# Quarter-array recurrence, u parts made two steps ahead, and other counts around the gate stage in a hybrid encoder kernel

## The chip, the cores and the metric

The kernel runs on one core of one Trainium2 chip. The metric is the time of one execution on the device, in microseconds. The parts of the core are called as in the profile: PE (TensorE, matrix products), PEld (its weight loads), DVE (VectorE), ACT (ScalarE), POOL (GpSimd), SP (SyncE, which here only issues transfers).

## The reference

The reference is two residual layers over 512 tokens of width 1024, with a final norm. Each layer has a mixer and a feed-forward part. What the change touches is in the two feed-forward parts and in the second layer's mixer.

The feed-forward part picks, per token and head, 16 of 16384 single-neuron experts, and adds them:

```python
top_s, pos = lax.top_k(cand.astype(jnp.float32), PEER_TOPK)
idx = jnp.take_along_axis(cand_idx, pos, axis=-1)
gate = jax.nn.softmax(top_s, axis=-1)
...
act = jax.nn.gelu(jnp.einsum('thkd,td->thk', u, xb), approximate=False)
out = jnp.einsum('thk,thkd->td', gb * act, ve)
```

Half of the second mixer is a recurrence per head (8 heads of 64), with a 64 x 64 state:

```python
def step(state, inp):
    r_t, w_t, k_t, v_t, kk_t, a_t = inp
    sa = jnp.einsum('bhvk,bhk->bhv', state, kk_t)
    state = (state * w_t[:, :, None, :] - sa[..., None] * (kk_t * a_t)[:, :, None, :]
             + v_t[..., None] * k_t[:, :, None, :])
    y = jnp.einsum('bhvk,bhk->bhv', state, r_t)
    return state, y
```

## The kernel before

The program is even mixer, feed-forward (`peer`, layer 0), odd mixer, `peer` (layer 1). Each engine carries out its instructions in the order of the program; what stands first and waits holds up all behind it on that engine.

**The feed-forward part** computes for 384 of the 512 tokens all 16384 experts densely, in 128 tiles of 128 experts: a "u tile" (`u_mm`, L1379) is 24 products of 128x128 by 128x384, three per slice of the contraction. The weights `ur` and the tokens are split into a high part and a low part (`uh`, L1369, made on ACT by L151; `ul`, L1376, on DVE), and `mm3` (L179) runs high by high (L182), high by token-low (L183) and low by token-high (L184). The result goes through a gelu on ACT into `act` tiles that stay, or into `acts` tiles (two buffers) that go out to memory (`ad`, the spill). The first `NB_ACT` = 15 tiles stay, the next `NB_SPILL` = 38 are spilled; the others come later. The 128 tokens that are left get their expert rows by indirect transfers (`g_fetch`, `g_work`).

While the u tiles run, DVE finds the best 16 (`level2`) and builds for the dense tokens the gates: per block of 16 tokens one-hot arrays `ohC`, `ohA`, and two `ohB` (L1606, four operations of 128x2048), which PE multiplies (`flush`, L1589, `gps`); ACT copies the result, and it is written to memory (`gd`). `background` (L1615) yields the cost of each piece, and a loop (L1633) puts in a `u_step` for every `G_STEP` = 4.2 of cost: it makes the low part of tile j + 1, loads the high part of tile j + 2, and multiplies tile j. When the gates are done (or up to `NB_LAST` tiles ahead of the end), the remaining tiles follow until 53 - 2, then the v stage opens and the last two run. This stretch is called the gate stage here, and the passage from the last gates to the first v product the handover.

**The v stage** (L1645 on) goes over the 128 tiles with 18 products each (`v_mm`, L1701, outputs `o`), weights split into `vh` and `vl`, and activations times gates (`Hf`, then `Hh` and `Hl`). The gates of 8 tiles are read back in one transfer `gt` (1536 KB). In the first 38 steps the spilled activations are read back (`a_load`), in the next 75 each step also makes one more u tile, and the last steps are v products alone. `units` (L1822) spreads the row work over these steps.

**The recurrence** (`odd_mixer`, L1106 to L1275) works on 8 chunks of 64 tokens. Two heads lie on the 128 partitions. Each operand is expanded to a block-diagonal 128x128 matrix with zeros beside the two heads' blocks (`expand`, L719, mostly on POOL), and `mm4` (L1114) runs four full 128x128 products for the four pairs of heads. `prep(c)` (L1118) makes for one chunk the inverse of a triangular matrix from blocks of 16 (`Xc`, `XTc`) by two levels, and the products that don't need the state; `step(c)` (L1187) runs the chain through the state: `psT` to `t1`, `psU` to `u`, `psS` to the new state, and `psY` to the output. `prep(c + 1)` and a group norm of chunks before are woven into the steps (L1259 on).

Of the kernel before, what the change touches and what calls it, by code (L numbers as in the profile page):

```python
# [25 lines left out]
P = 128  # L26
# [67 lines left out]
for _nm, _c in (("blk64", 128), ("mB", 128), ("mK", 256), ("lv16", 128), ("lv32", 128), ("hm", 2), ("rows", 4)):  # L94
    OC[_nm] = (_n, _c)
    _n += _c
# [3 lines left out]
def odd_const_array():  # L100
    c = np.zeros((P, NOC), np.float32)
    i = np.arange(P)
    r, q = i[:, None], i[None, :]
    same = r // 64 == q // 64
    rr, qq = r % 64, q % 64

    def put(nm, a):
        o, n = OC[nm]
        c[:, o:o + n] = a

    put("blk64", same / 64.0)
    put("mB", np.where(q < 64, 1.0 * (rr < qq), -1.0 * (rr <= qq)))
    put("mK", np.concatenate([same & (rr < qq), same & (rr <= qq)], 1))
    put("lv16", same & (rr // 32 == qq // 32) & (rr % 32 < 16) & (qq % 32 >= 16))
    put("lv32", same & (rr < 32) & (qq >= 32))
    put("hm", np.stack([i < 64, i >= 64], 1))
# [550 lines left out]
def odd_mixer(k):  # L667
# [8 lines left out]
    with ExitStack() as st:  # L676
# [40 lines left out]
        hm = o_("hm")  # L717

        def expand(e, dst, src):  # L719

            if e is nc.scalar:
                for h in range(2):
                    k.act(dst[:, :, 64 * h:64 * h + 64], src, AF.Copy, scale=hm[:, h:h + 1])
                return
            e.tensor_tensor(dst.rearrange("p a (h t) -> p a h t", h=2), src[:, :, None, :].to_broadcast([P, 4, 2, 64]),
                            hm[:, None, :, None].to_broadcast([P, 4, 2, 64]), op=ALU.mult)

        def gram(c, pb):
            tt = slice(64 * c, 64 * c + 64)
            b0 = pb.tile([P, 4, P], F32, name="b0", tag="b0", bufs=2)  # L730
            expand(nc.gpsimd, b0, be[:, :, tt])

            def rest():
                ps = bank4()
                for p in range(4):
                    mm(ps[:, p, :], b0[:, p, :], AR[:, p, :, tt], start=True, stop=True, skip_group_check=True)
# [10 lines left out]
        with ExitStack() as s1:  # L747
# [136 lines left out]
            with ExitStack() as s2:  # L884
# [40 lines left out]
                def grams(n):  # L925
                    if n >= 4:
                        gq.pop(0)()
                    if 2 <= n < 10:
                        gq.append(gram(n - 2, p3))
# [28 lines left out]
        def bc4(a):  # L958
            return a[:, None, :].to_broadcast([P, 4, P])

# [143 lines left out]
        for i in range(3):  # L1104
            ws.fetch(i)
        rs = ExitStack()  # L1106
        pw = rs.enter_context(sb("odw", 2))
        S, C = {}, {}
        Y = AR[:, :, 1]

        def t4(nm, n=1, bufs=2):
            return pw.tile([P, 4, n * P], F32, name=nm, bufs=bufs)

        def mm4(ps, l, r, start, stop):  # L1114
            for p in range(4):
                mm(ps[:, p, :], l[:, p, :], r[:, p, :], start=start and p == 0, stop=stop, skip_group_check=True)  # L1116

        def prep(c):  # L1118
            tt = slice(64 * c, 64 * c + 64)
            K0, B0 = t4("k0"), t4("b0")  # L1120
            AR0 = t4("ar", 2)
            X, XT = t4("x"), t4("xt")
            N1, N2 = t4("n1"), t4("n2", bufs=1)
            NB2 = t4("nb2")

            def level(dst, nm):
                for h in range(2):
                    f = slice(64 * h, 64 * h + 64)
                    (nc.vector if h and not c else nc.gpsimd).tensor_tensor(dst[:, :, f].rearrange("p a (b i) -> p a b i", b=4),
                                            Na[:, :, :, 4 * c:4 * c + 4].rearrange("p i b a -> p a b i"),  # L1130
                                            o_(nm)[:, None, f].rearrange("p a (b i) -> p a b i", b=4)
                                            .to_broadcast([P, 4, 4, 16]), op=ALU.mult)

            ve, ae = (nc.gpsimd, nc.gpsimd) if c else (nc.vector, nc.scalar)
            level(N1, "lv16")
            expand(ve, X, Xc[:, 4 * c:4 * c + 4, :])
            expand(ae, K0, ka[:, :, tt])
            expand(ve, XT, XTc[:, 4 * c:4 * c + 4, :])
            expand(nc.gpsimd, B0, be[:, :, tt])
            yield  # L1140
            expand(ae, AR0[:, :, 0:P], AR[:, :, 0, tt])
            level(N2, "lv32")
            expand(ve, NB2, Nr[:, c])
            expand(nc.gpsimd, AR0[:, :, P:], AR[:, :, 1, tt])
            KT, NT, VT = t4("kt"), t4("nt"), t4("vt")
            ps = bank4()
            for p in range(4):
                for s in range(2):
                    mm(ps[64 * s:64 * s + 64, p, :], vT[:, p, tt], ident, start=True, stop=True, skip_group_check=True)
            nc.vector.tensor_tensor(VT, ps, bc4(cst(k, "blk")), op=ALU.mult)  # L1150

            KK = t4("kk", 2)
            ps = bank4()
            for p in range(4):
                mm(ps[:, p, :], K0[:, p, :], AR[:, p, :, tt], start=True, stop=True, skip_group_check=True)
            for i in range(2):
                nc.vector.tensor_tensor(KK[:, :, i * P:i * P + P].rearrange("p a (h t) -> p a h t", h=2),
                                        ps[:, :, None, 64 * i:64 * i + 64].to_broadcast([P, 4, 2, 64]),
                                        o_("mK")[:, None, i * P:i * P + P].rearrange("p a (h t) -> p a h t", h=2)
                                        .to_broadcast([P, 4, 2, 64]), op=ALU.mult)  # L1160
            ps = bank4()
            mm4(ps, N1, X, True, True)
            Q = t4("q")
            k.act(Q, ps, AF.Copy)
            yield
            ps, ps2 = bank4(), bank4()
            mm4(ps, XT, Q, True, True)
            nc.vector.tensor_tensor(X, X, ps, op=ALU.subtract)
            mm4(ps2, Q, XT, True, True)
            nc.vector.tensor_tensor(XT, XT, ps2, op=ALU.subtract)  # L1170
            yield
            ps = bank4()
            mm4(ps, N2, X, True, True)
            Q = t4("q")
            k.act(Q, ps, AF.Copy)
            for src, dst, sgn in ((K0, KT, 1.0), (B0, NT, -1.0)):
                ps = bank4()
                for p in range(4):
                    nc.tensor.transpose(ps[:, p, :], src[:, p, :], ident)
                k.act(dst, ps, AF.Copy, scale=sgn)  # L1180
            yield
            ps = bank4()
            mm4(ps, Q, XT, True, True)
            nc.vector.tensor_tensor(XT, XT, ps, op=ALU.subtract)
            C[c] = (AR0, KK, KT, NT, VT, XT, NB2)

        def step(c):  # L1187
            AR0, KK, KT, NT, VT, XT, NB2 = C.pop(c)
            tt = slice(64 * c, 64 * c + 64)
            s0 = S.get(c - 1)  # L1190
            psT = bank4()
# [3 lines left out]
            t1 = t4("t1", bufs=1)  # L1195
            k.act(t1, psT, AF.Copy)
            psS, psY = bank4(), bank4()
            mm4(psS, KT, VT, True, False)
            mm4(psY, VT, KK[:, :, P:], True, False)
            se = None  # L1200
            if c:
                se = t4("se", bufs=1)
                nc.vector.tensor_tensor(se, s0, ec[:, :, c:c + 1].to_broadcast([P, 4, P]), op=ALU.mult)
            yield
            psU = bank4()
            mm4(psU, XT, t1, True, True)
            u = t4("u", bufs=1)
            k.act(u, psU, AF.Copy)
            if c:
                mm4(psY, s0, AR0[:, :, P:], False, False)  # L1210
            yield
            mm4(psS, NT, u, False, True)
            s1 = t4("S")
            if c == 0:
                nc.vector.tensor_tensor(s1, psS, ec[:, :, c:c + 1].to_broadcast([P, 4, P]), op=ALU.mult)
            else:
                for p in range(4):
                    nc.vector.scalar_tensor_tensor(s1[:, p, :], psS[:, p, :], ec[:, p, c:c + 1], se[:, p, :],
                                                   op0=ALU.mult, op1=ALU.add)
            S[c] = s1  # L1220
            mm4(psY, u, NB2, False, True)
            for s in range(2):
                h = slice(64 * s, 64 * s + 64)
                k.act(Y[h, :, tt], psY[h, :, 64 * s:64 * s + 64], AF.Copy)
# [35 lines left out]
        gn = iter(())  # L1260
        for c in range(8):
            nx = prep(c + 1) if c < 7 else iter(())
# [6 lines left out]
            drain(nx)  # L1269
# [4 lines left out]
        k.dump("Y", AR[:, :, 1])  # L1274
# [46 lines left out]
NB_ACT = 15  # L1321
NB_SPILL = 38
# [3 lines left out]
NB_LAST = 4  # L1326


def peer(k, layer):
    nc, tc = k.nc, k.tc  # L1330
    I = k.I
    with ExitStack() as st:
# [30 lines left out]
        def u_load(j):  # L1363
            if j < NE:
# [3 lines left out]
                h = up.tile([P, KD, P], F32R, name="uh", bufs=3)  # L1368
# [682 lines left out]
```

## Time and profile before

| | |
|---|---|
| median of 3 runs | 3352.92 us (3352.59 to 3361.28) |
| the profiled execution | 3354.57 us |
| its span, first to last instruction | 3352.8 us |
| PE busy | 3195.3 us, 95% |
| DVE busy | 2462.0 us, 73% |
| ACT busy | 1435.1 us, 43% |
| POOL busy | 990.4 us, 30% |
| mean granted clock of TensorE | 0.981 |

In rows of the timeline the columns are start, duration, engine, line, operation, output <- inputs, shapes and count, then in brackets the idle time before and what ended it. A product of fp32 operands shows as two matmul records, one of the faster split type (fp32r) as one. Rows of PE give a duration that overlaps the next row's: the distance of starts is the price. In rows of waits the numbers are the sum, the count and the longest.

### The profile page before, as it was taken

How to read it: one execution, taken by the hardware profiler on the slowest of the kernel's cores; microseconds unless marked ns; L12 is line 12 of the kernel's file. 1: busy time of each engine (PE TensorE's matmuls, PEld its weight loads, DVE VectorE, ACT ScalarE, POOL GpSimd, SP SyncE). 2: the span in 40 equal slices, each digit the busy share in tenths (PEclk: the TensorE clock that was granted, in tenths of full speed). 3: DMA queues.
4: the chain of work that ended last, by engine and by line, in shares of the span. 5: the costliest groups of instructions: out<-in, count | busy, mean ns of one | idle time of the engine just before them, and what ended most of it. 6: DMA issues, size and time to landing. Idle time of an engine off the chain costs nothing.

```text
span 3352.8 us, 53012 instructions
## 1 busy us (share of the span) xinstructions
PE 3195.3 (95%) x20560; PEld 2795.9 (83%) x20560; DVE 2462.0 (73%) x4771; ACT 1435.1 (43%) x1998; POOL 990.4 (30%) x785
## 2 busy tenths in 40 slices
PE   7999989999999999998999998989989999999998
PEld 5777888888899999986776897888877899999997
DVE  5246888957788888887565466788957788888886
ACT  3353357743333333334445334357743333333334
POOL 1004200013344444443122634200013344444442
PEclk9999999999999999999999999999999999999999
DMA  8524246699999999994520014246789999999984
GB/s 314 189 104 132 89 137 223 230 307 331 314 347 332 325 329 347 330 315 166 185 73 23 4 45 147 93 134 221 238 289 317 316 342 338 328 323 340 340 315 167
DMA packets 317117, 791.10 MB, mean 236 GB/s; under 512 B 23744, under 2 KB 158272, under 8 KB 304576
## 3 DMA queue, kind: packets, MB, share of 16 engines
q1 hardware_dynamic: 222416, 437.95, 38.2%
q0 software_dynamic: 75008, 274.78, 23.5%
q10 hardware_dynamic: 19440, 74.98, 6.0%
q8 instruction: 161, 2.64, 0.3%
q14 instruction: 92, 0.75, 0.1%
HBM read 713.92 MB, written 73.66 MB: 235 GB/s over the span
## 4 chain that ended last, share of the span: by engine, by line
PE 78%; DVE 9%; DMA 5%; ACT 5%; issue 2%; ACTq 0%; POOL 0%; SPq 0%; DVEq 0%; POOLq 0%
PE o L1701 27%; PE ups L184 9%; PE ups L182 9%; PE ups L183 9%; PE bk L1116 3%; PE bk L182 3%; PE bk L184 3%; PE bk L183 3%; DMA vr<-peer_vp 2%; PE qps L182 2%; PE qps L183 2%; PE qps L184 2%; DVE ul L1376 1%; PE gps L1589 1%; PE adaps L242 1%
## 5 line engine op out<-in xcount | busy, mean ns | idle before, releaser
L184 PE MATMUL ups<-phh,ul 128*128 128x384 f32 x2048 | 697.3, 340 | 48.9 <-DVE ul L1376 48.8
L182 PE MATMUL ups<-phh,uh 128*128 128x384 f32 x2048 | 699.0, 341 | 5.8 <-ACT acts L151 5.8
L1723 POOL DMA_INDIRECT row<-peer_u,xres x256 | 350.1, 1368 | 1173.8 <-PE gps L1589 604.3
L183 PE MATMUL ups<-phl,uh 128*128 128x384 f32 x2048 | 691.9, 338 | 0.0
L151 ACT ACTIVATE vh<-vr 128x1024 fp32r<-128x1024 f32 x254 | 269.7, 1062 | 545.3 <-issue 433.9
L1701 PE MATMUL o<-vh,Hh 128*128 128x512 f32 x1524 | 475.6, 393 | 18.3 <-ACT Hh L151 18.3
L1701 PE MATMUL o<-vh,Hl 128*128 128x512 f32 x1524 | 472.4, 391 | 0.0
L1701 PE MATMUL o<-vl,Hh 128*128 128x512 f32 x1524 | 472.3, 391 | 0.0
L1723 POOL DMA_INDIRECT row<-peer_v,xres x256 | 340.3, 1329 | 409.8 <-DVE xres L1739 314.3
L184 PEld LDWEIGHTS ups<-phh,ul 128*128 128x128 f32 x2048 | 389.6, 190 | 58.8 <-DVE ul L1376 58.8
L176 DVE TENSOR_TENSOR vl<-vr,vh 128x1024 fp32r<-128x1024 f32 x254 | 311.1, 1225 | 125.1 <-ACT vh L151 112.8
L182 PEld LDWEIGHTS ups<-phh,uh 128*128 128x128 f32 x2048 | 390.1, 191 | 12.3 <-ACT acts L151 6.4
L183 PEld LDWEIGHTS ups<-phl,uh 128*128 128x128 f32 x2048 | 389.7, 190 | 5.8
L1701 PEld LDWEIGHTS o<-vh,Hh 128*128 128x128 f32 x1524 | 282.8, 188 | 73.7 <-ACT Hh L151 25.7
L1701 PEld LDWEIGHTS o<-vl,Hh 128*128 128x128 f32 x1524 | 286.8, 188 | 62.8
L1701 PEld LDWEIGHTS o<-vh,Hl 128*128 128x128 f32 x1524 | 286.8, 188 | 61.8
L1376 DVE TENSOR_TENSOR ul<-ur,uh 128x1024 fp32r<-128x1024 f32 x256 | 312.0, 1219 | 26.5 <-ACT uh L151 17.9
L1742 DVE SCALAR_TENSOR_TENSOR gacc<-row,xres,gacc 128x1024 f32<-128x1024 f32 x256 | 327.7, 1280 | 2.3 <-DMA row<-peer_v,xres 1.6
L176 DVE TENSOR_TENSOR Hl<-Hf,Hh 128x384 fp32r<-128x384 f32 x254 | 141.9, 559 | 234.5 <-ACT Hh L151 234.5
L1739 DVE SCALAR_TENSOR_TENSOR xres<-row,xres 128x1024 f32<-128x1024 f32 x256 | 311.9, 1218 | 3.0 <-DMA row<-peer_u,xres 3.0
L151 ACT ACTIVATE uh<-ur 128x1024 fp32r<-128x1024 f32 x256 | 269.6, 1053 | 17.5 <-ACT acts L151 3.2
L151 ACT ACTIVATE act<-ups 128x384 f32<-128x384 f32 x180 | 88.5, 492 | 386.3 <-PE ups L184 386.2
(487 smaller groups left out, 4831.1 us busy)
## 6 DMA issues: line engine op xcount, KB each, us to landing
ur<-peer_uT SPq DMA_DIRECT2D x256, 512.0 KB
vr<-peer_vp SPq DMA_DIRECT2D x256, 512.0 KB
gt<-gd SPq DMA_DIRECT2D x32, 1536.0 KB
adaw<-ada_w SPq DMA_DIRECT2D x32, 1024.0 KB
wraw<-peer_wq SPq DMA_DIRECT2D x32, 512.0 KB
wraw<-od_w_in SPq DMA_DIRECT2D x30, 512.0 KB
ad<-acts ACTq DMA_DIRECT2D x76, 192.0 KB
act<-ad SPq DMA_DIRECT2D x76, 192.0 KB
```

What stands on the lines that cost most here:

```text
L151: return self.nc.scalar.activation(out, in_, func, **kw)
L176: (eng or k.nc.vector).tensor_tensor(lo, src, hi.bitcast(F32), op=ALU.subtract)
L182: mm(out, w[0], x[0], start=start, stop=False, skip_group_check=True)
L183: mm(out, w[0], x[1], start=False, stop=False, skip_group_check=True)
L184: mm(out, w[1], x[0], start=False, stop=stop, skip_group_check=True)
L242: nc.tensor.matmul(ps[32 * q:32 * q + 32], k.cact[:, d:d + 1].to_broadcast([P, 32]), w[:, d, q], start=d == 0, stop=d == KD - 1, skip_grou ...
L1116: mm(ps[:, p, :], l[:, p, :], r[:, p, :], start=start and p == 0, stop=stop, skip_group_check=True)
L1376: nc.vector.tensor_tensor(l, r, h.bitcast(F32), op=ALU.subtract)
L1701: mm(O_[t][b], w[:, ts], v[:, 512 * b:512 * b + 512], start=s, stop=e, skip_group_check=True)
L1723: nc.gpsimd.indirect_dma_start(out=r, out_offset=None, in_=I[f"peer_{kind}{layer}"], in_offset=bass.IndirectOffsetOnAxis(ap=eidx[:, c:c + ...
L1739: nc.vector.scalar_tensor_tensor(junk, r, 1.0, htok, op0=ALU.mult, op1=ALU.mult, accum_out=dots[:, c:c + 1])
L1742: nc.vector.scalar_tensor_tensor(acc, r, wts[:, c:c + 1], acc, op0=ALU.mult, op1=ALU.add)
```

## The change

Five things change together.

**Recurrence.** The block-diagonal expansion is gone. `heads` runs each pair of heads as two 64x64 products, one on partitions 0 to 63 and one on 64 to 127 of the array's rows and columns, both into one bank of PSUM. `prep(m)` now prepares two chunks at once (8 pairs of heads by chunk). The transposes of `ka`, `be` and `vT` are products with a 64x64 identity. The state update is an addition and a multiplication of 256 columns. The output has a tile of its own. The products `gram` ahead of it take the same form.

**u parts.** The low part is made two tiles ahead and the high part loaded three ahead, with one buffer more for each (`uh` 4, `ul` 3); before the scores end, one tile more is loaded and one more low part is made.

**Gates.** `ohA` has three buffers in place of two.

**Counts.** 13 activations stay (15), 42 are spilled (38), and `NB_LAST` is 6 (4).

**Gates read back.** `gt` is fetched when the v stage loads a tile that lies 6 ahead of it, not 3.

```diff
+        def heads(ps, l, r, start=True, stop=True):
+            for a in range(ps.shape[1]):
+                for g in range(2):
+                    h = slice(64 * g, 64 * g + 64)
+                    mm(ps[h, a, :], l(h, a), r(h, a), start=start and a == 0, stop=stop, skip_group_check=True)
...
-            mm4(psT, KK[:, :, 0:P], VT, True, c == 0)
+            psT = half()
+            heads(psT, lambda h, p: KK[h, a0 + p, 0:64], of(VT, a0), True, c == 0)
             if c:
-                mm4(psT, AR0[:, :, 0:P], s0, False, True)
+                heads(psT, lambda h, p: AR[h, p, 0, tt], of(s0), False, True)
...
-            mm4(psU, XT, t1, True, True)
+            heads(psU, of(XT, a0), of(t1))
...
+            if c:
+                nc.vector.tensor_tensor(s1, psS, s0, op=ALU.add)
+            nc.vector.tensor_tensor(s1, s1 if c else psS, ec[:, :, c:c + 1].to_broadcast([P, 4, 64]), op=ALU.mult)
...
-            nx = prep(c + 1) if c < 7 else iter(())
+            if c % 2 == 0 and c < 6:
+                nx = prep(c // 2 + 1)
...
-NB_ACT = 15
-NB_SPILL = 38
+NB_ACT = 13
+NB_SPILL = 42
...
-NB_LAST = 4
+NB_LAST = 6
...
-                h = up.tile([P, KD, P], F32R, name="uh", bufs=3)
+                h = up.tile([P, KD, P], F32R, name="uh", bufs=4)
...
-                l = up.tile([P, KD, P], F32R, name="ul")
+                l = up.tile([P, KD, P], F32R, name="ul", bufs=3)
...
-                if m in (10, 12, 14):
-                    u_load(m // 2 - 5)
-                if m in (11, 13):
-                    u_low(m // 2 - 5)
+                if m in (8, 10, 12, 14):
+                    u_load(m // 2 - 4)
+                if m in (9, 11, 13):
+                    u_low(m // 2 - 4)
...
-                C, A = (wk.tile([P, GB // 2, P, 2], F16, name=nm, bufs=n) for nm, n in (("ohC", 1), ("ohA", 2)))
+                C, A = (wk.tile([P, GB // 2, P, 2], F16, name=nm, bufs=n) for nm, n in (("ohC", 1), ("ohA", 3)))
...
         def u_step(j):
-            u_low(j + 1)
-            u_load(j + 2)
+            u_low(j + 2)
+            u_load(j + 3)
             u_mm(j, j >= NB_ACT)
...
-                g_load(j + 3)
+                g_load(j + 6)
```

What the change moves on PE in the recurrence, first one chunk as it stood (from the preparation of the next chunk's `vT` on; `bk` is the PSUM result, `S` the state, `x` and `xt` the inverse, 4 products to a row):

```order
L1149 MATMUL bk<-consts,xres 64x128 x8
L1155 MATMUL bk<-AR,k_17590 128x128 x4
L1116 MATMUL bk<-x,n_17595 128x128 x4
L1116 MATMUL bk<-u,nt 128x128 x4
L1116 MATMUL bk<-nb_17471,u 128x128 x4
L1116 MATMUL bk<-q,xt 128x128 x4
L1116 MATMUL bk<-xt,q 128x128 x4
```

The same engine now, in the first chunk's step with the preparation of the next two chunks between its parts (`lv` is the masked level, `Xc` and `XTc` the inverse):

```order
L723 MATMUL bk<-kk,vt 64x64 x8
L723 MATMUL bk<-Xc,lv_17593 64x64 x16
L723 MATMUL bk<-consts,xres 64x64 x16
L723 MATMUL bk<-t_17573,XTc 64x64 x8
L723 MATMUL bk<-q,XTc 64x64 x16
L723 MATMUL bk<-XTc,q 64x64 x16
L723 MATMUL bk<-consts,ka 64x64 x16
L723 MATMUL bk<-u,nt 64x64 x8
L723 MATMUL bk<-Nr,u 64x64 x8
L723 MATMUL bk<-AR,ka 64x128 x16
```

Four full products have become eight quarter products in a step and sixteen in a preparation, which now serves two chunks and stands in every other chunk only.

On DVE in the gate stage of layer 0, at the first block that finds no free buffer (`ul` is a tile's low part, `ge`, `pf` and `c` belong to the search for the best 16), before:

```order
L1376 TENSOR_TENSOR ul<-ur,uh 128x1024 [waits DMAHW6_49,PE_49,Activation_49]
L1606 TENSOR_TENSOR ohC<-xres,pT 128x2048 [waits DVE_49]
L1606 TENSOR_TENSOR ohA<-xres,pT 128x2048 [waits PE_49]
L1526 TENSOR_TENSOR ge<-tv 128x128
L1529 CAST pf<-tp 128x128
```

and now:

```order
L1355 TENSOR_TENSOR ul<-ur,uh 128x1024 [waits DMAHW7_49,PE_49,Activation_49]
L1585 TENSOR_TENSOR ohC<-xres,pT 128x2048 [waits DVE_49]
L1585 TENSOR_TENSOR ohA<-xres,pT 128x2048
L1505 TENSOR_TENSOR ge<-tv 128x128
L1508 CAST pf<-tp 128x128
L1512 TENSOR_TENSOR c_4784<-pf,xres 128x2048 [waits DVE_49]
L1355 TENSOR_TENSOR ul<-ur,uh 128x1024 [waits DMAHW0_49,PE_49,Activation_49]
L1585 TENSOR_TENSOR ohB<-ohC,pT 128x2048 [waits PE_49] x2
```

The wait for PE has left `ohA` and stands at the two `ohB`, behind the next `ul`.

More of the change, by code (lines that the diff above doesn't have):

```diff
@@ L93 @@
 _n = 0
-for _nm, _c in (("blk64", 128), ("mB", 128), ("mK", 256), ("lv16", 128), ("lv32", 128), ("hm", 2), ("rows", 4)):
+for _nm, _c in (("blk64", 128), ("mB", 128), ("mK", 128), ("lv16", 64), ("lv32", 64), ("rows", 4)):
     OC[_nm] = (_n, _c)
@@ L716, in odd_mixer, with of, gram @@
         Nr = po3.tile([P, 8, 4, 64], F32, name="Nr")
[L717 to L728, printed above, removed]
+        def heads(ps, l, r, start=True, stop=True):
[3 more added lines that the diff above has]
+                    mm(ps[h, a, :], l(h, a), r(h, a), start=start and a == 0, stop=stop, skip_group_check=True)
+        def of(t, a0=0):
+            return lambda h, a: t[h, a0 + a]
+        def gram(c):
             tt = slice(64 * c, 64 * c + 64)
-            b0 = pb.tile([P, 4, P], F32, name="b0", tag="b0", bufs=2)
-            expand(nc.gpsimd, b0, be[:, :, tt])
             def rest():
                 ps = bank4()
-                for p in range(4):
-                    mm(ps[:, p, :], b0[:, p, :], AR[:, p, :, tt], start=True, stop=True, skip_group_check=True)
+                heads(ps, lambda h, p: be[h, p, tt], lambda h, p: AR[h, p, :, tt])
                 for p in range(4):
@@ L1105, in odd_mixer @@
             ws.fetch(i)
+        Y = pn.tile([P, 4, T], F32, name="y")
         rs = ExitStack()
@@ L1108, in odd_mixer @@
         S, C = {}, {}
[L1109 to L1139, printed above, removed]
-            yield
[L1141 to L1155, printed above, removed]
-            for i in range(2):
[L1157 to L1163, printed above, removed]
@@ L1164, in prep @@
             k.act(Q, ps, AF.Copy)
             yield
[L1166 to L1180, printed above, removed]
@@ L1196, in step @@
+            t1 = t8("t1", 4)
             k.act(t1, psT, AF.Copy)
[L1197 to L1203, printed above, removed]
+            psS, psY = half(), half()
+            heads(psS, of(KT, a0), of(VT, a0), True, False)
+            heads(psY, of(VT, a0), lambda h, p: KK[h, a0 + p, 64:], True, False)
@@ L1214, in step @@
[L1214 to L1219, printed above, removed]
+            heads(psS, of(NT, a0), of(u), False, True)
+            s1 = t8("S", 4)
+            if c:
+                nc.vector.tensor_tensor(s1, psS, s0, op=ALU.add)
@@ L1220, in step @@
+            nc.vector.tensor_tensor(s1, s1 if c else psS, ec[:, :, c:c + 1].to_broadcast([P, 4, 64]), op=ALU.mult)
             S[c] = s1
[L1221 to L1224, printed above, removed]
+            heads(psY, of(u), lambda h, p: Nr[h, c, p], False, True)
+            k.act(Y[:, :, tt], psY, AF.Copy)
             yield
@@ L1671, in v_load @@
                     h, l = (up.tile([P, KD, P], F32R, name=nm, bufs=b).rearrange("p a b -> p (a b)")
-                            for nm, b in (("uh", 3), ("ul", 2)))
+                            for nm, b in (("uh", 4), ("ul", 3)))
                 else:
```

90 lines of the change are left out of this document (66 added, 24 removed).

## Prediction

> **What bounds the kernel now.** I read the page first, then PE's waits, then the stages that the change touches by windows and timeline.
>
> ```profile
> span 3352.8 us, 53012 instructions
> PE 3195.3 (95%) x20560; PEld 2795.9 (83%) x20560; DVE 2462.0 (73%) x4771; ACT 1435.1 (43%) x1998; POOL 990.4 (30%) x785
> PE ups L184 <- DVE ul L1376: 48.8, 28, 4.1
> PE ups L184 <- DVE ul L1376: 24.0, 14, 4.1
> ```
>
> PE is busy 95% of the span, so time is won only by less PE work or by filling its gaps. The first wait row is the whole run: the largest gap is PE standing before the third product of an expert tile until VectorE has made the tile's low part (`ul`). The second row is the same wait from 2170 to 2600 us: half belongs to each of the two FFN layers, so a layer is costed once and doubled. Three places follow: the stretch where gates are built (gate stage), the handover to the v stage, and the recurrence.
>
> The gate stage of layer 0, first its start on PE, then one stall inside it (DVE rows, then PE):
>
> ```profile
> 404.81 0.33 PE L184 MATMUL ups<-phh,ul 128*128 128x384 f32 x1
> ...
> 405.68 0.34 PE L183 MATMUL ups<-phl,uh 128*128 128x384 f32 x1
> 410.14 0.69 PE L184 MATMUL ups<-phh,ul 128*128 128x384 f32 x1 [4.13 <-DVE ul L1376]
> 410.63 0.52 PE L182 MATMUL ups<-phh,uh 128*128 128x384 f32 x1
> 410.95 0.52 PE L183 MATMUL ups<-phl,uh 128*128 128x384 f32 x1
> 416.07 0.40 PE L184 MATMUL ups<-phh,ul 128*128 128x384 f32 x1
> 460.86 1.22 DVE L1606 TENSOR_TENSOR ohC<-xres,pT 128x2048 f16<-128x2048 f16 x1
> 467.15 1.23 DVE L1606 TENSOR_TENSOR ohA<-xres,pT 128x2048 f16<-128x2048 f16 x1 [5.08 <-PE gps L1589]
> 469.89 1.22 DVE L1376 TENSOR_TENSOR ul<-ur,uh 128x1024 fp32r<-128x1024 f32 x1
> 471.17 0.69 PE L184 MATMUL ups<-phh,ul 128*128 128x384 f32 x1 [2.73 <-DVE ul L1376]
> ```
>
> Unhindered, five products take 0.87 us (404.81 to 405.68), 0.174 each, so a tile of 24 takes 4.17. After the 4.13 us wait they start 0.32 us apart until 416.07, 18 of them: another 18 x 0.146 = 2.6 us. So the start costs 6.7. The lower rows show a circle: DVE stands 5.08 us before `ohA` because both its buffers wait for PE's gate products; `ul` is queued behind, and when it comes PE has waited 2.73 us for it.
>
> The gate stage by windows, and DVE's own wait from 437 to 685 (columns: from:to, length, PE, PEld, DVE, ACT, POOL busy, clock, DMA share, GB/s):
>
> ```profile
> 437.00:530.00 93.00, 79.75 (x585) 76.09 (x584) 78.17 (x160) 56.28 (x65) 0.00 (x0) 0.93 0.50 170
> 530.00:600.00 70.00, 66.77 (x512) 63.91 (x511) 63.65 (x132) 49.04 (x56) 0.00 (x0) 1.00 0.65 218
> 600.00:685.00 85.00, 78.89 (x652) 75.09 (x651) 76.87 (x150) 62.28 (x72) 0.00 (x0) 1.00 0.69 236
> DVE ohA L1606 <- PE gps L1589: 23.4, 11, 5.1
> PE gps L1589 <- DVE ohB L1606: 5.3, 4, 1.8
> ```
>
> In these 248 us PE idles 248 - 225.4 = 22.6 and loses 7% of 93 = 6.5 to the lower clock: its work is 219 us. DVE's work is 78.2 + 63.7 + 76.9 = 218.7. Neither can get below that, and the two are equal.
>
> **Gates: `ul` and `uh` one step earlier, third `ohA`.** Before scores end, `ul` of tile 2 is now made too (one 1.22 us operation more there, which at worst delays the next ones by as much), so the 6.7 us at the start go. Inside the stage PE has a whole tile (4.17 us) in hand when DVE comes back, more than the 2.73 it lacked. But `ohB` still has four buffers, two per block, released by the same gate products: the order shows the wait leaving `ohA` and standing at `ohB`, one or two operations later. Queued behind it are `ohC` and the next `ul`; that `ul` is now for a tile two further on. With DVE and PE work both at 219 us, queues of finite depth will not reach 219. I keep the 5.3 us before the first gate products and 4 us of new DVE-to-PE waits: 228 instead of 248, a gain of 20 (between 5, if the wait only changes its name, and 27). The number of u tiles among the gates is the same, as the order of PE has it. Per layer 6.7 + 20 = 26.7.
>
> **Handover: 13 resident, 42 spilled, 6 behind the gates.** PE's last gate products and first v products, with the waits between (layer 0; the acts row of layer 1; then ACT and DVE):
>
> ```profile
> 681.09 3.85 PE L1589 MATMUL gps<-ohB,ohA 128*128 128x128 f16 x64
> 684.74 0.42 PE L182 MATMUL ups<-phh,uh 128*128 128x384 f32 x1
> 703.47 0.45 PE L182 MATMUL ups<-phh,uh 128*128 128x384 f32 x1 [1.83 <-ACT acts L151]
> 708.11 0.69 PE L184 MATMUL ups<-phh,ul 128*128 128x384 f32 x1 [4.02 <-DVE ul L1376]
> 714.34 0.63 PE L1701 MATMUL o<-vh,Hh 128*128 128x512 f32 x2
> 2470.11 0.45 PE L182 MATMUL ups<-phh,uh 128*128 128x384 f32 x1 [3.94 <-ACT acts L151]
> 702.93 0.49 ACT L151 ACTIVATE acts<-ups 128x384 f32<-128x384 f32 x1 [7.42 <-DMA ad<-acts]
> 712.06 0.56 DVE L1682 TENSOR_TENSOR Hf<-act,gt 128x384 f32<-128x384 f32 x1 [4.01 <-DMA gt<-gd]
> ```
>
> Five tiles lie between, 20.9 us of work in 29.6 (684.74 to 714.34): 8.7 lost. Two more tiles move here out of the v stage. The first `Hf` waits for the gates to come back from memory, 27.3 us after the last gate product; seven tiles are 29.2, so that wait is covered. The 4.02 us wait for `ul` goes, since the load of the first v tile, which stood ahead of it on ACT and DVE, now follows two tiles later. The wait for the spill buffer stays (its two `acts` buffers wait for a DMA behind the gate writes): 1.83 and 3.94. Seven tiles plus about 2 to 4: 6 us gained per layer (between 3 and 8).
>
> Four more activations go out and back (192 KB each way) per layer and the first part of the v stage has 42 steps instead of 38; the products are the same in sum. I charge 1.5 us. Gates read at +6 instead of +3 issue the same transfers behind the same `vr` fetch of their step: nothing. The row work of the expert rows spreads over 73 instead of 75 long steps: hidden by PE, nothing.
>
> **Recurrence.** PE from its first product to the next stage, with the window of one steady chunk and ACT's copy of one result:
>
> ```profile
> 1859.08 1.09 PE L1149 MATMUL bk<-consts,xres 128*64 128x128 f32 x16
> 1872.85 1.06 PE L1116 MATMUL bk<-vt,kk 128*128 128x128 f32 x8
> 1891.55 1.09 PE L1149 MATMUL bk<-consts,xres 128*64 128x128 f32 x16
> 1892.57 1.16 PE L1155 MATMUL bk<-AR,k 128*128 128x128 f32 x8
> 1893.57 1.06 PE L1116 MATMUL bk<-x,n 128*128 128x128 f32 x8
> 1894.46 1.06 PE L1116 MATMUL bk<-u,nt 128*128 128x128 f32 x8
> 1906.58 1.09 PE L1149 MATMUL bk<-consts,xres 128*64 128x128 f32 x16
> 1990.44 0.47 PE L182 MATMUL bk<-cath,wh 128*128 128x512 f32 x1
> 1891.55:1906.58 15.03, 14.98 (x138) 14.41 (x137) 5.89 (x11) 4.27 (x9) 10.71 (x12) 1.00 0.01 2
> 1970.62 0.60 ACT L151 ACTIVATE u<-bk 128x512 f32<-128x512 f32 x1 [2.08 <-PE bk L1116]
> 219.22 1.10 PE L242 MATMUL adaps<-adaw,cact 128*32 128x64 f32 x64
> 220.25 0.50 PE L615 MATMUL zA<-sph,ntrir 128*128 128x512 f32 x1
> ```
>
> The stage takes 131.4 us (1859.08 to 1990.44), 15.03 a chunk, PE full in it (14.98). A group of four products is 8 records of 128 columns in 0.893 us (1893.57 to 1894.46), 0.112 each. The new group is 16 records of 64 columns on quarter arrays, two heads on different rows and columns. A record of half the columns is taken as 0.056. Two column halves do run side by side: 16 records of 128 columns in 1.02 us (1891.55 to 1892.57), 0.064 each against 0.112. If the quarters do too, a group takes 8 x 0.056 = 0.446.
>
> A pair of chunks is 36 groups by the order (20 to prepare, 16 for the two steps; the two of KK are double, being 128 columns wide): 16.1 us. The three group norms inside, at 3 x 0.99 with a change of array shape at 0.1, add 3.0 each. Prepare of the first pair: 20 x 0.446 = 8.9 after 2.4 us until DVE is free, about 11.5. Three pairs with the next pair's preparation: 48.3, and two group norms 6: 54.3. The last pair: 16 groups, 7.1, and 3.0: 10.1. On top come waits that 7 us of PE work per chunk no longer hides: a chunk's chain is three groups, two copies on ACT (0.60 at 512 columns, now 256) and two DVE operations, some 3.8 us, and copies and updates queue behind the preparation's. I take 1 us a chunk, 8 (between 0 and 16). Sum 84: a gain of 47 (39 to 55). POOL's 10.71 us a chunk vanish; they were hidden.
>
> The grams keep their price (16 records of 128 columns, two at a time, are 0.893 as before); 16 changes of shape at 0.1 cost 1.6.
>
> **Sum.** 47 - 1.6 + 2 x (26.7 + 6 - 1.5) = 108. The profiled execution took 3354.57 (span 3352.8), 1.65 above the median of 3352.92: from the median, 3245.
>
> **Rivals.** *The quarters take turns.* Both heads of a product write one PSUM bank, from different rows of the array, and no row of this profile shows two row groups at work together. Then a group takes 0.893: prepare 19, pairs 3 x 32.1 + 6, the last 17.3, waits 3: 142, a loss of 10 in place of a gain of 47: 3302. The Trainium skill ("TensorEngine Tiling (Array Packing)", Gotcha 1: PSUM Pressure) says that different row tiles cannot access the same PSUM bank simultaneously, which would bring this about; the column halves above share a bank and overlap, but they share their rows. Chance 16%.
>
> *The wait only moves to `ohB`.* DVE stands there as long as it stood at `ohA`, PE waits as before: 5 instead of 20 per layer, 3275. Against it: `ul` is then already there for one more tile. Chance 14%.
>
> *Slower: a narrow record costs as much as a wide one,* 0.112 us, say for its weight load. A group is 1.79, a chunk pair 64: prepare 36, 3 x 64.3 + 6, last 31.6, together 267, 136 more than now; less 62 in the FFN layers and with the grams' 1.6: 3428. It decides from about 0.08 us a record on. Against it: 64 records of 64 columns on quarter columns take 1.03 us (219.22 to 220.25), 0.016 each. Chance 4%.
>
> **How the numbers follow.** Forecast 3245 at 64%, its own range 3219 (recurrence 55; gates 27, handover 8) to 3275 (39; 12, 3). The range reaches from there up to the turn-taking case: 3219 to 3303. A measurement tells about 0.3% (10 us) from no change. Faster 0.94; within 0.3% 0.02 (turns, `ohB` and a worse v stage together); slower 0.04.
>
> **What would show it.** Right: records of 64x64 tiles 0.028 apart; 1859 to 1990 shrunk to about 84 us; PE's wait for `ul` under 10 us in the whole run, and a wait of DVE for gate products at `ohB`; no 4 us gap at the start of a gate stage; the gate stage some 27 us shorter. Wrong: 0.056 us between records, `ul` waits above 30 us, or new waits for `vr` and `act` at the head of the v stage.

## The result and the profile after

The changed kernel takes 3274.0 us (median of 4 runs, 3270.8 to 3280.1) against 3352.8 before: 0.976 of the time, 95% interval 0.974 to 0.978. The forecast was 3245; of the 108 us that it summed up, some 79 came. The profiled execution took 3280.1 with a span of 3277.9, 74.9 less than before's 3352.8. Of the executions in the experiments one of gates5, at 3535 us with a granted clock of 0.83, is left out as a slow one.

The page of the changed kernel, and rows of PE's waits over the whole run:

```profile
span 3277.9 us, 55074 instructions
PE 3136.6 (96%) x21696; PEld 2739.6 (84%) x21696; DVE 2429.6 (74%) x4725; ACT 1420.2 (43%) x1974; POOL 901.7 (28%) x696
```

```profile
PE o L1680 <- ACT Hh L151: 40.1, 17, 6.6
...
PE gps L1568 <- DVE ohB L1585: 11.0, 10, 2.6
...
PE pkT L1545 <- DVE pk L1479: 5.7, 2, 2.9
PE bk L723 <- DVE lv L1121: 5.3, 3, 3.2
```

The row that led before, PE waiting for `ul` (48.8 us), is gone altogether. In its place stands PE in the v stage, waiting for `Hh`: 40.1 us, where it was 18.3, and the forecast had nothing for this growth. Behind it lies ACT's wait for the v tile `vr`. Both waits before, and ACT's after:

```profile
PE o L1701 <- ACT Hh L151: 18.3, 15, 2.7
ACT vh L151 <- DMA vr<-peer_vp: 31.7, 12, 4.2
```

```profile
ACT vh L151 <- DMA vr<-peer_vp: 42.1, 10, 7.8
```

The recurrence on PE: the first product of the first preparation, one group of it that is 128 columns wide and the product behind it, the first products of the first step and of the seventh, and the first product of the projection behind:

```profile
1842.15 1.21 PE L723 MATMUL bk<-Xc,lv 64*64 64x64 f32 x32 [3.17 <-DVE lv L1121]
...
1848.41 1.92 PE L723 MATMUL bk<-AR,ka 64*64 64x128 f32 x32
1850.16 1.10 PE L723 MATMUL bk<-Xc,lv 64*64 64x64 f32 x32
...
1852.96 0.63 PE L723 MATMUL bk<-vt,kk 64*64 64x64 f32 x16
1853.43 0.63 PE L723 MATMUL bk<-vt,kt 64*64 64x64 f32 x16
...
1912.89 0.68 PE L723 MATMUL bk<-vt,kk 64*64 64x64 f32 x16
...
1925.71 0.48 PE L182 MATMUL bk<-cath,wh 128*128 128x512 f32 x1
```

Sixteen records on quarter arrays take 0.47 us (1852.96 to 1853.43), 0.029 each. Those of 128 columns take 0.055 (1848.41 to 1850.16, 32 records), half the 0.112 of a record of 128 columns on the full array: the two heads of a product run side by side. The stage is 83.6 us from its first product to the projection. But this first product waits 3.2 us for DVE, where the first one of before came without a wait. Counted with this wait it is 86.7 us, where it was 131.4.

The gate stage of layer 0 by windows (columns as in the prediction), and all of DVE's waits in it:

```profile
437.00:530.00 93.00, 90.21 (x692) 87.75 (x691) 88.75 (x225) 63.00 (x74) 0.00 (x0) 0.98 0.60 211
530.00:600.00 70.00, 69.08 (x555) 66.97 (x554) 69.28 (x117) 55.73 (x64) 0.00 (x0) 1.00 0.72 254
600.00:657.00 57.00, 56.30 (x487) 54.61 (x486) 56.18 (x93) 46.97 (x53) 0.00 (x0) 1.00 0.72 248
```

```profile
DVE ul L1355 <- ACT uh L151: 3.5, 1, 3.5
```

PE is busy 215.6 and DVE 214.2 of 220 us: the two work almost without a gap, and DVE waits for no gate product at all, neither at `ohA` nor at `ohB` (in layer 1 for 1.6 us at `ohB`).

The handover of layer 0 on PE: the last gate products, the wait for a spill buffer, the first v product:

```profile
655.27 1.94 PE L1568 MATMUL gps<-ohB,ohA 128*128 128x128 f16 x31 [0.70 <-DVE ohB L1585]
...
675.64 0.44 PE L182 MATMUL ups<-phh,uh 128*128 128x384 f32 x1 [1.72 <-ACT acts L151]
...
690.50 0.73 PE L1680 MATMUL o<-vh,Hh 128*128 128x512 f32 x2 [2.10 <-ACT Hh L151]
```

Seven u tiles, 29.2 us of work, fill 33.3 (657.2 to 690.5).

Then the head of the v stage, by windows: the first 38 steps or so of each layer before, and the first 42 or so now.

```profile
714.34:875.76 161.42, 157.68 (x685) 129.17 (x685) 117.86 (x168) 61.10 (x79) 45.97 (x29) 0.99 0.93 311
2479.70:2640.00 160.30, 153.38 (x665) 125.34 (x665) 115.11 (x164) 59.07 (x77) 46.85 (x29) 0.99 0.90 300
```

```profile
690.50:876.33 185.83, 171.05 (x717) 139.09 (x718) 126.46 (x179) 64.25 (x83) 50.43 (x32) 0.95 0.86 288
2396.03:2580.00 183.97, 165.07 (x690) 134.29 (x690) 120.90 (x172) 62.01 (x80) 47.07 (x30) 0.94 0.85 286
```

PE's idle time there rose from 3.7 and 6.9 us to 14.8 and 18.9, and the granted clock fell from 0.99 to 0.95 and 0.94. One such stall, step 12 of layer 0, followed back: SP's transfers, ACT's split of the v tile, PE.

```profile
724.40 0.43 SPq L1633 DMA_DIRECT2D gt<-gd  x1
727.62 7.26 SPq L1372 DMA_DIRECT2D act<-ad  x1
734.99 0.37 SPq L1642 DMA_DIRECT2D vr<-peer_vp  x1
```

```profile
743.08 1.06 ACT L151 ACTIVATE vh<-vr 128x1024 fp32r<-128x1024 f32 x1 [6.70 <-DMA vr<-peer_vp]
...
780.25 1.06 ACT L151 ACTIVATE vh<-vr 128x1024 fp32r<-128x1024 f32 x1 [3.42 <-DMA vr<-peer_vp]
```

```profile
746.53 1.22 PE L1680 MATMUL o<-vh,Hh 128*128 128x512 f32 x2 [5.49 <-ACT Hh L151]
747.55 1.05 PE L1680 MATMUL o<-vl,Hh 128*128 128x512 f32 x2
...
783.71 0.72 PE L1680 MATMUL o<-vh,Hh 128*128 128x512 f32 x2 [2.21 <-ACT Hh L151]
```

SP issues the read of eight tiles' gates in 0.43 us, but its next issue, the read of a spilled activation, takes 7.26. Only then, at 734.99, does it issue the v tile `vr`, which is there 8.0 us later; ACT has waited 6.70 for it. `Hf` and `Hh` of that step are queued behind `vl` and `vh`, so PE waits for `Hh`. Its wait is ACT's less 1.21: 5.49 for 6.70, 2.21 for 3.42, and likewise at the other stalls. Up to 1.2 us of lateness is free, the rest is paid in full, and with a slow clock behind (granted 0.51 from 744 to 751 us): rows of two products start 0.85 to 1.0 us apart after 746.53 instead of 0.46, so that this step takes 11.9 us in place of 4.08.

### The profile page after: what moved, and what is told of

The parts are those of the page before. It is cut to its first block, busy times and chain, and to the rows that moved or that the text cites. A ratio compares the mean times of both kernels' runs of the same rounds, so it can differ in the third digit from the quotient of the medians.

```text
span 3277.9 us, 55074 instructions
## 1 busy us (share of the span) xinstructions
PE 3136.6 (96%) x21696; PEld 2739.6 (84%) x21696; DVE 2429.6 (74%) x4725; ACT 1420.2 (43%) x1974; POOL 901.7 (28%) x696
## 4 chain that ended last, share of the span: by engine, by line
PE 64%; DVE 6%; DMA 4%; ACT 3%; issue 2%; SPq 0%; ACTq 0%; DVEq 0%
PE o L1680 27%; PE ups L182 8%; PE ups L184 8%; PE ups L183 8%; DMA vr<-peer_vp 2%; PE bk L723 2%; PE bk L182 2%; PE bk L184 2%; PE bk L183 2%; PE gps L1568 1%; PE qps L182 1%; PE qps L183 1%; PE qps L184 1%; ACT vh L151 1%; DMA ur<-peer_uT 1%
## 5 line engine op out<-in xcount | busy, mean ns | idle before, releaser
L184 PE MATMUL ups<-phh,ul 128*128 128x384 f32 x2048 | 688.5, 336 | 0.0
L1680 PE MATMUL o<-vh,Hh 128*128 128x512 f32 x1524 | 480.2, 396 | 40.1 <-ACT Hh L151 40.1
L182 PEld LDWEIGHTS ups<-phh,uh 128*128 128x128 f32 x2048 | 386.1, 189 | 10.8 <-ACT acts L151 5.1
L151 ACT ACTIVATE uh<-ur 128x1024 fp32r<-128x1024 f32 x256 | 269.6, 1053 | 24.2 <-DMA ur<-peer_uT 7.5
```

The lines of the kernel that those rows point to most:

```text
L151: return self.nc.scalar.activation(out, in_, func, **kw)
L182: mm(out, w[0], x[0], start=start, stop=False, skip_group_check=True)
L184: mm(out, w[1], x[0], start=False, stop=stop, skip_group_check=True)
L1680: mm(O_[t][b], w[:, ts], v[:, 512 * b:512 * b + 512], start=s, stop=e, skip_group_check=True)
```

## The experiments

In these series the kernel before ran at medians of 3355 to 3357 us, so kernels are compared by their ratio to it. Where the text gives a difference to the changed kernel in us, it is that of the medians; by the ratios these gains are 3 to 5 us larger. "ACT for `vr`" and "PE for `Hh`" are those engines' waits in the whole profiled execution, in us.

| kernel | median | ratio (95% interval) | ACT for `vr` | PE for `Hh` |
|---|---|---|---|---|
| changed kernel | 3274.0 | 0.976 (0.974 to 0.978) | 42.1 | 40.1 |
| rec_only | 3315.0 | 0.986 (0.983 to 0.990) | 34.0 | 21.5 |
| u_one | 3291.4 | 0.980 (0.978 to 0.983) | 34.3 | 34.0 |
| ohA2 | 3282.7 | 0.978 (0.975 to 0.980) | 33.7 | 34.3 |
| xd12 | 3266.9 | 0.973 (0.971 to 0.975) | 30.7 | 33.0 |
| gates7 | 3279.1 | 0.976 (0.974 to 0.978) | 53.9 | 41.8 |
| gates5 | 3270.8 | 0.973 (0.970 to 0.976) | 37.1 | 33.7 |
| gates3 | 3248.8 | 0.967 (0.966 to 0.969) | 24.2 | 19.7 |
| gtact | 3242.7 | 0.966 (0.964 to 0.968) | 24.2 | 14.7 |
| rows42 (two executions) | 3238.5 | 0.964 (0.961 to 0.967) | 2.2 | 18.8 |
| split4 | 3234.6 | 0.964 (0.962 to 0.965) | 8.4 | 9.9 |
| split6 | 3232.3 | 0.963 (0.960 to 0.965) | 0.8 | 9.3 |
| last4 | 3234.8 | 0.963 (0.961 to 0.965) | 0.4 | 6.8 |

The theory: the part that fell short is the head of the v stage, where the moved read of the gates makes `vr` late. Rivals: the four more spilled activations, the read of x in step 8, the sum of the traffic, or a smaller gain elsewhere.

**The recurrence alone (rec_only).** All constants and distances of the feed-forward part as before.

```diff
-NB_ACT = 13
-NB_SPILL = 42
+NB_ACT = 15
+NB_SPILL = 38
...
-                g_load(j + 6)
+                g_load(j + 3)
```

> The kernel before with the quarter-array recurrence and grams alone; all of the FFN layers as before. The trace after shows the recurrence stage about 87 us long where it was 131.4. Theory (the recurrence gave what the prediction said, the missing 30 us are in the v stages): the stage is again 85 to 89 us and the whole kernel 3307 to 3312. Rival (part of the recurrence's gain is given back elsewhere, for instance in the grams or in the projection behind it): 3318 or more.

The stage on PE, its first product and the projection's:

```profile
1869.74 1.98 PE L723 MATMUL bk<-Xc,lv 64*64 64x64 f32 x32 [3.18 <-DVE lv L1121]
...
1953.23 0.48 PE L182 MATMUL bk<-cath,wh 128*128 128x512 f32 x1
```

It is 83.5 us again, 86.7 with the wait ahead of its first product. The median, 3315, is over the 3312 of the theory, but before ran high as well: the ratio of 0.9863 is 46 us of 3352.8, with an interval of 35 to 57. The recurrence's part of the forecast (45 with the grams) is borne out within this interval; the feed-forward parts then brought some 33 of the forecast 62.

**Gates three steps ahead again (gates3),** all else as in the changed kernel.

```diff
-                g_load(j + 6)
+                g_load(j + 3)
```

> The changed kernel with the gates read 3 steps ahead again, as before. Theory A (the moved read of the gates, 1536 KB on the queue that also carries the v rows, makes vr late at the head of the v stage): PE's waits for Hh in the first 42 v steps fall from 16.9 and 18.9 us per layer to before's 3.7 and 6.9, about 16 us a layer with the clock lost behind each: 3240 to 3250. Theory B (the four more spilled activations do it, being read back in 42 steps rather than 38): no change, 3270 to 3280, waits as in the changed kernel.

SP's transfers around the second read of the gates, and ACT's wait for `vr` in the whole run:

```profile
740.70 0.46 SPq L1633 DMA_DIRECT2D gt<-gd  x1
743.82 4.33 SPq L1372 DMA_DIRECT2D act<-ad  x1
748.26 0.44 SPq L1642 DMA_DIRECT2D vr<-peer_vp  x1
```

```profile
ACT vh L151 <- DMA vr<-peer_vp: 24.2, 10, 4.2
```

3248.8: this one number in the diff costs 25 us of the 30 that were missing. PE's waits in the heads, behind the first v product, are 8.2 and 2.7 us, with the 42 spilled activations still there, so theory A stands and theory B falls. The issue behind the gates' read still takes 4.33, but no longer 7.26.

**Each read of the gates in four parts (split4), six parts (split6).** In split6 the parts go out eight to three steps ahead, and x comes in three reads.

```diff
                 if j < NE and j % GJ == 0:
-                    g = vp.tile([P, TD // GB, GJ, GB], F32, name="gt")
-                    nc.sync.dma_start(g, gd[:, :, j:j + GJ, :].rearrange("b p j t -> p b j t"))
-                    GG[j // GJ] = g
+                    GG[j // GJ] = vp.tile([P, TD // GB, GJ, GB], F32, name="gt")
+                    g_part(j, 0, 24 if not j else 6)
+                elif 8 <= j < NE and j % GJ < 4:
+                    g_part(j - j % GJ, 6 * (j % GJ), 6 * (j % GJ) + 6)
+
+            def g_part(j, lo, hi):
+                nc.sync.dma_start(GG[j // GJ][:, lo:hi], gd[lo:hi, :, j:j + GJ, :].rearrange("b p j t -> p b j t"))
```

> The changed kernel with each read of the gates cut into four reads of 384 KB, six, five, four and three steps ahead. If vr is late because one read of 1536 KB stands in front of it (its issue and the next one's hold SyncE's queue for 3 to 8 us), the stalls every eight steps go: PE's waits for Hh in the first 42 v steps under 5 us a layer, 3232 to 3245. If it is the sum of the traffic (86% of the DMA engines there), the waits spread and stay: 3265 to 3280.

> The changed kernel with each read of the gates cut into six reads of 256 KB, eight to three steps ahead, and the read of x[:, 5:8] cut into three, in steps 13, 21 and 29. If what is left of PE's wait for Hh with four reads (9.9 us in the whole run) comes from the size of the reads and from x, it falls below 4 us: 3224 to 3231. If four reads already fit into the slack: 3231 to 3238, as with four.

In split6, SP's transfers at one such place, and ACT's wait for `vr` in the whole run:

```profile
722.66 0.43 SPq L1638 DMA_DIRECT2D gt<-gd  x1
725.29 0.32 SPq L1372 DMA_DIRECT2D act<-ad  x1
725.71 0.39 SPq L1646 DMA_DIRECT2D vr<-peer_vp  x1
```

```profile
ACT vh L151 <- DMA vr<-peer_vp: 0.8, 2, 0.4
```

The issue behind a part takes 0.32 us here (0.3 to 0.5 throughout the heads), and `vr` is on time. split4 came at 3234.6, inside the theory's range; split6 at 3232.3 with PE's wait for `Hh` at 9.3, not under 4: with four parts there was next to nothing left to win, as the rival said. Both beat the changed kernel by some 40 us and before by 120. So the sum of the traffic is not the limit: the heads of split6, by windows, move more bytes per second (the last column) than before's 311 and 300.

```profile
691.95:860.00 168.05, 166.68 (x735) 137.56 (x735) 129.68 (x183) 66.05 (x84) 58.55 (x35) 1.00 0.95 327
2373.35:2545.00 171.65, 169.41 (x746) 139.91 (x747) 132.11 (x187) 67.64 (x86) 58.08 (x36) 1.00 0.95 326
```

A further kernel changed `NB_LAST` from 6 to 4 in split6:

> The version with six reads of the gates and three of x, with four u tiles instead of six kept behind the last gates (so two more stand among the gates). Theory (five tiles, 20.9 us, do not cover the 27 us until the gates are back, seven do): PE waits about 6 us more a layer ahead of the first v product, and the two tiles lengthen the gate stage by 8.3: gate stage plus handover 3 to 8 us a layer longer than 247.7 and 248.7, 3238 to 3248. Rival (the two tiles fill PE's gaps among the gates): the same sum of stages, 3229 to 3236.

That gave the same program, instruction for instruction: the loop that puts u tiles among the gates runs out of gate work before it reaches this limit. The experiment says nothing of the handover, and nothing of what it expected; it is a second measurement of split6, at 3234.8 (ratio 0.9633 beside 0.9627). In the change, too, this constant had no part: the seven tiles behind the gates come from the 55 that the other two counts add up to.

**The read of x in step 13 instead of 8 (xd12).**

```diff
-                if j == 8:
+                if j == 13:
                     nc.gpsimd.dma_start(k.x[:, 5:8, :], xd[:, 5:8, :])
```

> The changed kernel with the read of x[:, 5:8] that GpSimd issues in v step 8 put into step 13. The read of the gates now goes out in step 9 instead of 12, right behind it. Theory C (these two reads together make the long stall at step 12, 5.5 and 6.6 us of wait with 2 to 3 more of slow clock): that stall falls to the size of the others, 3.5 us: 3262 to 3268. Theory A (the gates' read alone): the stall at step 12 stays above 5 us, 3270 to 3280.

The stall at step 12 shrank: ACT's wait there is 3.54 us instead of 6.70 in layer 0, 4.06 instead of 7.84 in layer 1. In time that is 7 us by the medians, with intervals that overlap. So the read of x, which six steps ahead meets the gates' read (steps 8 and 9) and three ahead does not (8 and 12), is a part of it, and not the larger.

**Five and seven steps ahead (gates5, gates7):** the same line with 5 and with 7.

> The changed kernel with the gates read 5 steps ahead, so that the reads go out in v steps 10, 18, 26 and so on instead of 9, 17, 25 (three steps ahead it was 12, 20, 28). What is asked is why 6 steps ahead is worse than 3. Theory (nearness to the read of x in step 8): only the read in step 10 still meets it, the stall behind it is smaller than at 6 ahead and the later ones are like those at 6 ahead: ACT's waits for vr 30 to 38 us in the run, 3262 to 3270. Rival (the place of the read among the row reads, whose pattern repeats about every seven steps): no order by the distance, every value from 20 to 45 us can come, and the stalls of the later reads change too.

> The changed kernel with the gates read 7 steps ahead, in v steps 8, 16, 24 and so on: the same step as the read of x. Theory (nearness to the read of x): the stall behind step 8 is as long as at 6 ahead or longer, the others the same: ACT's waits for vr 38 to 48 us, 3272 to 3285. Rival (place among the row reads): the stalls of the later reads change as well, 3245 to 3275.

ACT's wait for `vr` in gates7:

```profile
ACT vh L151 <- DMA vr<-peer_vp: 53.9, 13, 7.8
```

The waits rise with the distance: 24.2, 37.1, 42.1, 53.9 us at 3, 5, 6 and 7, one profile each; in time, 5, 6 and 7 cannot be told apart. At 5, 6 and 7 the stall nearest the read of x is ACT waiting 6 to 8 us in each layer, as nearness to x would have it. But the later stalls, far from x, are longer too (in layer 1 at 7 ahead 5.84, 4.00 and 6.38, at 3 ahead 2.17, 0.93 and 3.27), which that theory did not say. Why they are stays open.

**Rows later (rows42).** The expert rows' reads begin in step 41 and the work on them in step 42. In the changed kernel three reads go out ahead of step 0, and the work begins in step 4.

```diff
-            g_fetch(3)
...
-            units = [0 if j < 4 else 2.5 if j < NB_SPILL else 8.5 if j < NB_SPILL + NE - ju else 4 for j in range(LAST)]
+            units = [0 if j < NB_SPILL else 8.5 if j < NB_SPILL + NE - ju else 4 for j in range(LAST)]
...
+                if j == NB_SPILL - 1:
+                    g_fetch(3)
```

> The changed kernel with the row work of the expert rows (512 KB a row, by GpSimd's queue) begun in v step 42 rather than step 4, so that no row is read while the head of the v stage reads back activations and gates. Theory (the gates' read makes vr late because rows are read beside it): PE's waits for Hh in the first 42 steps fall from 16.9 and 18.9 us to under 8 a layer. Rival (the gates' read does it by itself, standing ahead of vr in one queue): 13 us or more stay. The whole time has no clear sign here, since the same row work then falls on fewer long steps: 3240 to 3285.

ACT's wait for `vr` in the whole run:

```profile
ACT vh L151 <- DMA vr<-peer_vp: 2.2, 4, 0.9
```

PE's waits in the heads are 2.2 and 1.8 us: the gates' read in one piece on SP's queue does next to no harm where no rows are read beside it. It takes both. SP's longest issue in the heads is then 3.2 us, where it was 7.9. The time, 3238.5, is a gain of 36 us; some is paid back later, where PE now waits some 15 us for `Hh` (18.8 in the run, 4.0 of it in the heads).

**Gates on another queue (gtact).** One read of 1536 KB as in the change, but issued by ScalarE (all but the first of a layer).

```diff
-                    nc.sync.dma_start(g, gd[:, :, j:j + GJ, :].rearrange("b p j t -> p b j t"))
+                    (nc.scalar if j else nc.sync).dma_start(g, gd[:, :, j:j + GJ, :].rearrange("b p j t -> p b j t"))
```

> The changed kernel, gates still in one read of 1536 KB six steps ahead, but issued by ScalarE on its own queue, which carries nothing else in the v stage; vr and the spilled activations stay on SyncE's queue. Theory (vr is late because it stands behind the gates' read in one queue, whose rate the row reads beside it take down): with the queue apart, ACT's waits for vr fall from 42.1 us to under 12 and PE's stalls with them: 3232 to 3245. Rival (the DMA engines themselves are full while gates and rows are read): 30 us of waits for vr or more stay, 3265 to 3280.

ACT's wait for `vr`, and PE's in the head of layer 0 (690 to 860):

```profile
ACT vh L151 <- DMA vr<-peer_vp: 24.2, 17, 3.1
```

```profile
PE o L1680 <- ACT Hh L151: 3.9, 6, 1.4
```

The time, 3242.7, is where the theory put it; the waits are between the two expectations. They are as long in sum as in gates3, but they are 17 instead of 10, and of each only what exceeds some 1.2 us is paid. SP's longest issue in the heads is 1.5 us. Hence what made the stalls long was the read's place on SP's queue. That the gates' read still slows `vr` through the transfer engines, which they share, is the likely reading of the waits that stay; no run shows it apart. The Trainium skill ("DMA: Bandwidth & Descriptors", Issuing engines are not separate DMA queues) says that transfers of different issuing engines run on the same 16 engines, and that issuing from several saves only the issuing time, usually small. The first half fits the 24.2 us that stay; the time saved was not small here, as it is 31 us.

**The gate stage by halves (u_one, ohA2):** u parts one step ahead with the third `ohA` (before the scores end and in the v stage, too, as before the change), and u parts two ahead with two `ohA`.

```diff
         def u_step(j):
-            u_low(j + 2)
-            u_load(j + 3)
+            u_low(j + 1)
+            u_load(j + 2)
...
```

```diff
-                C, A = (wk.tile([P, GB // 2, P, 2], F16, name=nm, bufs=n) for nm, n in (("ohC", 1), ("ohA", 3)))
+                C, A = (wk.tile([P, GB // 2, P, 2], F16, name=nm, bufs=n) for nm, n in (("ohC", 1), ("ohA", 2)))
```

> The changed kernel with the parts of a u tile made one step ahead again (two tiles before the scores end, not three), the third ohA kept. Theory (it is the low part made one tile earlier that covers PE; the third ohA alone moves DVE's wait to ohB): PE's wait for ul comes back, 15 to 24 us a layer, and the first gate product to the last takes 230 to 240 us instead of 215 to 218: 3300 to 3325. Rival (the third ohA does the work): no wait for ul over 5 us a layer, 3274 to 3285.

> The changed kernel with two ohA buffers, u parts two steps ahead kept. Theory (the earlier low part is what counts): DVE waits for gate products at ohA, but PE's wait for ul stays under 5 us a layer and the gate stage grows by less than 4 us: 3274 to 3282. Rival (the third buffer does the work): 10 us or more a layer, 3295 to 3315.

PE's wait for `ul` in u_one (whole run) and DVE's wait for gate products there (437 to 700):

```profile
PE ups L184 <- DVE ul L1355: 17.7, 15, 4.1
```

```profile
DVE ohB L1585 <- PE gps L1568: 1.5, 1, 1.5
```

PE's wait for `ohB` in ohA2 (whole run) and DVE's for gate products (437 to 700):

```profile
PE gps L1568 <- DVE ohB L1585: 19.5, 14, 2.7
```

```profile
DVE ohA L1585 <- PE gps L1568: 8.2, 3, 3.5
```

From the first gate product to the last it is 239.3 and 238.0 us in the two layers of before, 218.4 and 219.6 with the third `ohA` alone, 224.0 and 223.9 with the earlier u parts alone, and 215.1 and 218.4 with both. Neither expectation held in full. Each half breaks the circle of the prediction (DVE waits for PE's gate products while PE waits for DVE's `ul`) by itself, and within the gate stage the third buffer does more than the earlier low part. With the buffer alone the wait did not move to `ohB`: 1.5 us stand there, against 23.4 at `ohA` before. Counted with the handover behind it, the two halves come out alike: 251.8 and 255.4 us in u_one, 253.6 and 253.3 in ohA2, 248.4 and 250.5 with both. In ohA2 PE finds the spill buffers free in the handover, which is 29.6 and 29.3 us long, against 33.4 and 35.8 in u_one and 33.3 and 32.1 with both. In the whole, ohA2 cannot be told from the changed kernel (the intervals overlap), but its waits for `Hh` were 6 us shorter, which hides a part of the difference. u_one's interval barely meets that of the changed kernel: there PE's wait of 4.1 us for `ul` at the start of each gate stage is back, and gate stage and handover together are 3.3 and 4.9 us longer.

## Why the prediction was right, and where it was not

By stages of the profiled executions, in us, layer 0 and layer 1 apart:

| stretch | forecast | measured |
|---|---|---|
| up to the first gate product (layer 1: from the projection behind the recurrence) | -6.7, -6.7 | -3.6, -1.1 |
| first to last gate product | -20, -20 | -24.2, -19.7 |
| handover, with 8.3 us of u tiles added | +2.3, +2.3 | +3.9, +1.9 |
| v stage, with 8.3 us of u tiles fewer | -6.8, -6.8 | +5.5, +8.8 |
| v stage of layer 0 to the recurrence (grams) | +1.6 | -1.8 |
| recurrence, with the wait ahead of its first product | -47 | -44.6 |
| sum | -108 | -74.9 |

The sum of the last column is the difference in span. The 33 us between the columns are about 28 from the v stage, 9 from the start of the gate stage and 2 from the recurrence, less what the rest brought more.

*Recurrence: right.* 86.7 against 84, and the parts agree, so this was not luck: sixteen records of a quarter array take 0.47 us where 0.446 was reckoned. The parts: 3.2 of waiting and 10.8 for the first preparation (11.5 with 2.4 of waiting), 59.9 for the three pairs (54.3 and 6 of the 8 us of waits), 12.8 for the last (10.1 and the other 2). The rivals of turns (0.056 a record) and of a price that doesn't shrink (0.112) fall at 0.029. The Trainium skill ("TensorEngine Tiling (Array Packing)", Gotcha 1: PSUM Pressure), by which different row tiles cannot access one PSUM bank at once, differs from the trace here: two heads on different rows (and different columns) of the array write one bank side by side, at 0.029 us a record.

*Gates: the size right, the reason half wrong.* The gain of 20 came, and no wait for `ul` is left. But DVE's wait did not move to `ohB`; it vanished, but for 1.6 us in layer 1. The prediction took the order of the waits in the program for the waits themselves, and rested on the earlier low part where the third buffer alone does as much (218.4 and 219.6 us in u_one). That the 4 us of new waits which it allowed left it so close is in part luck. The rival that the wait moves to `ohB` falls.

*Start of the gate stage: too much.* 6.7 us were promised to each layer. Kernels with the same code up to there reach their first gate product between 441.9 and 445.5 us, so what came, 3.6, can hardly be told from nothing. The wait for `ul` went, but PE waits 2.9 us for `pk` instead (the row in PE's waits above, once per layer). In u_one, which makes one low part fewer there, this row is missing. The prediction had the delay by the added low part at 1.22 us at worst, and left it out of the sum.

*Grams: no loss shows.* The 1.6 us did not come. The stretch is 1.8 us shorter, and nearly all of this is one group of 14 products ahead of the recurrence that ran at about half rate before (4.0 us) and not now (2.3).

*Handover: right.* 4.4 and 6.4 us won beside the two tiles' work, against 6.

*The v stage: the step that failed.* "Gates read at +6 instead of +3 issue the same transfers behind the same `vr` fetch of their step: nothing", and 1.5 us for the rest. What the runs showed: the transfers are the same, but it is not the `vr` fetch ahead of the gates' read that suffers, it is the one behind it. One step's issue stands 3 to 8 us behind a read of 1536 KB while rows are read beside it; how long depends on what else is under way, and `vr` has only 1.2 us to spare. With the moved read each of the eight stalls in the heads is longer than in gates3; the nearness to the read of x is a part of the reason, the rest stays open. Put back, the read returned 25 us; cut into pieces, 40. The four more spilled activations, which the 1.5 us were for, cost nothing that shows: in split6 they are all there, and PE waits 1.4 and 3.6 us in the heads. The prediction named this sign as one that would prove it wrong ("new waits for `vr`"), but gave it no price and no chance of its own; before's profile already had ACT waiting 31.7 us for `vr`, most of it in the same place. That the forecast still came within 1% of the measured time is no merit of this term: the other terms were large enough to carry its error.

## What to carry to other kernels

A large read on a queue is paid for by the transfers behind it: before moving one, look at how long the next issue on that queue takes, and at how much slack its consumer has. Where the slack is small (here 1.2 us), many small reads in the gaps are worth more than one early read. And a circular wait between two engines can be broken at either end; a buffer more at the first wait may do it alone.

## What the runs showed of the hardware that was not expected

- An issue on SP's queue took up to 7.9 us behind a 1536 KB read of the gates (0.43 us to issue itself) with row reads by GpSimd under way, up to 3.2 without those, and 0.3 to 0.5 behind a read of 256 KB.
- A wait of 5.5 us on PE was followed by some ten products at half the rate (two in 0.85 to 1.0 us instead of 0.46): it cost 7.8 us in all.
- Products on opposite quarters of the array (64 rows by 64 columns each) that write one PSUM bank ran side by side: 0.029 us a record of 64 columns and 0.055 for one of 128, where the full array took 0.112 for one of 128.
